# Moving the staged weights of a fused decoder layer by 320 bytes against its activations

## The chip, the core and the metric

The kernel runs on one core of a Trainium2 chip. A core has five engines that run side by side: TensorE multiplies matrices, VectorE and ScalarE work element by element, GpSimd does a few odd jobs, and SyncE here only starts transfers. All read their operands from an on-chip memory of 128 partitions (SBUF); an address below is an offset in bytes along a partition, the same in all 128. TensorE has two kinds of instruction: a weight load (PEld in the rows) reads the stationary operand, a 128x128 block, and a matmul (PE) then reads the moving operand column by column and adds the products into an accumulator memory (PSUM). The metric is device microseconds for one execution, lower being better; the time is the median of several executions.

## What is computed

One layer of a decoder for 512 tokens of width 2048, in float32: a normalisation, one input projection, three token mixers (a gated recurrence A, a sparse attention B, a chunked spatial gating C), one output projection, a second normalisation, and a gated feed-forward part of width 5632 with a short convolution.

```python
h = rms_norm(x, norm_mix)
proj = h @ w_in                                   # 2048 x 6992
a_q, a_f, a_i, a_g, b_q, b_ckv, idx_q, idx_k, idx_w, c_uv = split_cols(proj, IN_SIZES)
out_a = hgrn2_mixer(a_q, a_f, a_i, a_g, lb, a_out_gain)
out_b = dsa_mixer(b_q, b_ckv, idx_q, idx_k, idx_w, w_uk, w_uv, kv_gain, rel_bias)
out_c = gmlp_mixer(c_uv, gmlp_w, gmlp_b)
x = x + concatenate([out_a, out_b, out_c]) @ w_out
h = rms_norm(x, norm_ffn)
a = causal_depthwise_conv3(h @ w_up) + conv_b     # 2048 x 11264
x = x + (silu(a[..., :D_FF]) * a[..., D_FF:]) @ w_down
return rms_norm(x, norm_final)
```

Nearly all of the work is the four matrix products with `w_in`, `w_out`, `w_up` and `w_down`.

## The kernel before

**Tiling.** Activations stand transposed: a tile is 128 features by 512 tokens. Weights come from memory in blocks of 128 by up to 1024 (`stage`, L76): SyncE starts the transfer into `raw`, ScalarE rounds it to `hi` (L82), VectorE makes the rest `lo` (L83). Activations are split into a high and a low part in the same way (`xh`/`xl`, `mh`/`ml`, `hh`/`hl`, `hidh`/`hidl`). Each product of a weight block and an activation tile is then three matmuls (`step`, L94 to 98): high by high, high weights by low activations, low weights by high activations. In `step` the weight block is the stationary operand (128 columns of 4 bytes, 512 bytes of each partition) and the activation tile the moving one (512 columns, 2048 bytes). In `stream` (L204 to 211) it is the other way round: a 128-column slice of the activation tile is stationary and the weights move.

**Stages, in order of time.** The first product (`pia`, weights `wiw`, 336 columns for each of 16 input tiles, L199 to 226) runs while the input arrives. Then come the projections (`proj`, `moving`), between them the three mixers, then the output projection (`wo`), then four groups of the feed-forward part, each with its up-projection (`up`, L793, moving operands `hh`/`hl`) and its down-projection (moving operands `hidh`/`hidl`).

**Addresses.** Tiles are given out by pools, and a pool lies behind the one opened before it. `const` comes first, then `act` (32 tiles of 2048 bytes: `xh`, `xl`, later `mh`, `ml`, `hidh`, `hidl`), `res` (16 tiles of 2048 bytes), `wp` (2 `raw`, 4 `hi`, 4 `lo`, 4096 bytes each), and behind `wp` the pools of the phases: `tp` and `ts` for the mixers, later `hp` (30 of the 32 tiles `hh`/`hl`) and `lp` (`wl_hi`, `wl_lo`). A tile `pad` of 192 bytes in `const` (L183) makes `act` begin at 21504, a multiple of 512. As all sizes up to `ts` are multiples of 512, `act`, `res`, `wp`, `tp`, `hp` and `lp` all begin at a multiple of 512, and so does every 128-column weight block in them. In what follows, the **gap** of a matmul is the start of its moving operand less the start of its stationary one, modulo 512. It is 0 for 10128 of the 10236 matmuls of the split kind. The other 108 are in the first product, where the moving block of an input tile is 1344 bytes wide, so that the blocks of one staged tile begin 0, 1344 and 2688 bytes into it: 60 matmuls have a gap of 320 and 48 one of 128.

```python
PADF = 48
    act = ctx.enter_context(tc.tile_pool(name="act", bufs=1))
    res = ctx.enter_context(tc.tile_pool(name="res", bufs=1))
    wp = ctx.enter_context(tc.tile_pool(name="wp", bufs=1))
    ...
    pad = const.tile([P, PADF], F32, name="pad")
    DVE.memset(pad, 0.0)
```

**Order.** Each engine runs its own instructions in the order in which they stand; waits on other engines are put in by the framework. Staging is given a high priority, so it stands as early as its buffers allow. On TensorE, ten matmuls on a tile of ones (`warm`, L181) stand ahead of the first product.

Of the kernel before, what the change touches and what calls it, by code (L numbers as in the profile page):

```python
# [8 lines left out]
F32 = mybir.dt.float32  # L9
# [6 lines left out]
P = 128  # L16
# [25 lines left out]
U_IQ, U_CKV, U_F, U_Q, U_BQ, U_CU, U_AG = 0, 8, 10, 16, 22, 28, 32  # L42
N_UNITS = 38
NL = 4
PADF = 48

C_NMIX, C_NFFN, C_NFIN, C_LB, C_AGAIN, C_KVG, C_CW, C_CB = 0, 16, 32, 48, 54, 55, 57, 321
N_CONST = 409
# [3 lines left out]
def trunk_kernel(ctx: ExitStack, tc: tile.TileContext, xT, consts, onehot, relb, gw, gb, wk, wv,  # L52
                 wst, wai, wiw, wcv, wo, wu, wd, outT):
    nc = tc.nc
    PE, ACT, DVE, POOL = nc.tensor, nc.scalar, nc.vector, nc.gpsimd

    const = ctx.enter_context(tc.tile_pool(name="const", bufs=1))
    act = ctx.enter_context(tc.tile_pool(name="act", bufs=1))
    res = ctx.enter_context(tc.tile_pool(name="res", bufs=1))
    wp = ctx.enter_context(tc.tile_pool(name="wp", bufs=1))  # L60
    psum = ctx.enter_context(tc.tile_pool(name="psum", bufs=1, space=bass.MemoryType.PSUM))
    dram = ctx.enter_context(tc.tile_pool(name="dram", bufs=1, space=bass.MemoryType.DRAM))

# [116 lines left out]
    for i in range(10):  # L180
        PE.matmul(warm, ones, ones, start=(i == 0), stop=(i == 9))  # L181

    pad = const.tile([P, PADF], F32, name="pad")  # L183
    DVE.memset(pad, 0.0)
    gmx = const.tile([P, KT], F32, name="gmx")
    ACT.dma_start(gmx, consts[:, C_NMIX:C_NMIX + KT])
    for k in range(KT):
# [755 lines left out]
```

## Time and profile before

| | us |
|---|---|
| time, median of 3 runs | 2303.12 (2302.98 to 2303.28) |
| time of the profiled execution | 2303.14 |
| its span, first to last instruction | 2301.4 |
| TensorE busy (matmul) | 2273.6 |
| TensorE busy (weight load) | 1915.3 |
| VectorE busy | 1216.4 |
| ScalarE busy | 878.7 |
| GpSimd busy | 86.1 |

The span is what the instructions of the trace cover; 1.7 us of the profiled execution lie around it. A matmul's duration in the profile (389 ns for 512 columns) covers its whole way through the engine; the next begins long before it ends. What a matmul costs in a dense row of them is the distance from its start to the start of the next, called its **pitch** below. Starts are printed to 0.01 us, so a pitch is best read over many matmuls: by the count in a stretch, or by the first and last start of a row.

### The profile page before, as it was taken

How to read it: one execution, taken by the hardware profiler on the slowest of the kernel's cores; microseconds unless marked ns; L12 is line 12 of the kernel's file. 1: busy time of each engine (PE TensorE's matmuls, PEld its weight loads, DVE VectorE, ACT ScalarE, POOL GpSimd, SP SyncE). 2: the span in 40 equal slices, each digit the busy share in tenths (PEclk: the TensorE clock that was granted, in tenths of full speed). 3: DMA queues.
4: the chain of work that ended last, by engine and by line, in shares of the span. 5: the costliest groups of instructions: out<-in, count | busy, mean ns of one | idle time of the engine just before them, and what ended most of it. 6: DMA issues, size and time to landing. Idle time of an engine off the chain costs nothing.

```text
span 2301.4 us, 27200 instructions
## 1 busy us (share of the span) xinstructions
PE 2273.6 (99%) x10788; PEld 1915.3 (83%) x10788; DVE 1216.4 (53%) x1992; ACT 878.7 (38%) x1272; POOL 86.1 (4%) x150
## 2 busy tenths in 40 slices
PE   8999999999999999999999999999999999999998
PEld 7988889888888888888888888888888888888887
DVE  7689576667675335444334444334544433454446
ACT  6536566755564324333223333222333222333224
POOL 4010000000011110000000000000000000000001
PEclk9999999999999999999999999999999999999999
DMA  5323222222233332332333332333233233323233
GB/s 180 110 89 131 92 78 74 74 71 89 83 124 116 99 98 94 96 97 84 96 107 100 101 97 88 94 98 110 93 100 97 83 95 110 101 94 99 71 113 110
DMA packets 72816, 226.49 MB, mean 98 GB/s; under 512 B 9220, under 2 KB 11674, under 8 KB 72688
## 3 DMA queue, kind: packets, MB, share of 16 engines
q1 hardware_dynamic: 67824, 211.40, 29.3%
q0 software_dynamic: 4720, 13.35, 1.7%
q8 instruction: 84, 1.38, 0.3%
q14 instruction: 44, 0.36, 0.1%
q10 hardware_dynamic: 144, 0.01, 0.0%
HBM read 220.50 MB, written 6.18 MB: 98 GB/s over the span
## 4 chain that ended last, share of the span: by engine, by line
PE 94%; DVE 2%; ACT 2%; DMA 1%; issue 1%; POOL 0%; DVEq 0%; ACTq 0%; POOLq 0%
PE pj L96 24%; PE pj L97 24%; PE pj L98 24%; PE mx L97 3%; PE mx L96 3%; PE mx L98 3%; PE pmv L209 1%; PE pmv L210 1%; PE pmv L211 1%; PE pa L444 1%; ACT hi L82 1%; DMA x<-in_xT_dram 0%; DVE lo L83 0%; PE psc L288 0%; PE ptr L642 0%
## 5 line engine op out<-in xcount | busy, mean ns | idle before, releaser
L82 ACT ACTIVATE hi<-raw 128x1024 fp32r<-128x1024 f32 (+5 forms) x438 | 420.3, 960 | 996.1 <-PE pj L97 764.0
L83 DVE TENSOR_TENSOR lo<-raw,hi 128x1024 fp32r<-128x1024 f32 (+5 forms) x438 | 483.1, 1103 | 459.7 <-ACT hi L82 459.3
L96 PE MATMUL pj<-hh,hi 128*128 128x512 f32 x1408 | 547.8, 389 | 0.0
L98 PE MATMUL pj<-hh,lo 128*128 128x512 f32 x1408 | 547.8, 389 | 0.0
L97 PE MATMUL pj<-hh,hi 128*128 128x512 f32 x1320 | 513.5, 389 | 0.0
L98 PEld LDWEIGHTS pj<-hh,lo 128*128 128x128 f32 x1408 | 264.3, 188 | 54.8
L96 PEld LDWEIGHTS pj<-hh,hi 128*128 128x128 f32 x1408 | 264.3, 188 | 54.7
L97 PEld LDWEIGHTS pj<-hh,hi 128*128 128x128 f32 x1320 | 247.8, 188 | 51.6
L96 PE MATMUL pj<-xh,hi 128*128 128x512 f32 (+1 forms) x608 | 232.2, 382 | 0.9 <-ACT ia L254 0.9
L97 PE MATMUL pj<-xl,hi 128*128 128x512 f32 (+1 forms) x608 | 231.7, 381 | 0.0
L98 PE MATMUL pj<-xh,lo 128*128 128x512 f32 (+1 forms) x608 | 231.0, 380 | 0.0
L787 DVE TENSOR_TENSOR a<-pj,rs 128x512 f32<-128x512 f32 x88 | 60.8, 691 | 291.4 <-PE pj L98 289.4
L96 PEld LDWEIGHTS pj<-xh,hi 128*128 128x128 f32 x608 | 114.2, 188 | 19.2 <-ACT ia L254 1.1
L98 PEld LDWEIGHTS pj<-xh,lo 128*128 128x128 f32 x608 | 114.2, 188 | 18.0
L97 PEld LDWEIGHTS pj<-xl,hi 128*128 128x128 f32 x608 | 114.3, 188 | 17.8
L96 PE MATMUL pj<-hidh,hi 128*128 128x512 f32 x320 | 124.5, 389 | 0.0
L97 PE MATMUL pj<-hidl,hi 128*128 128x512 f32 x320 | 124.5, 389 | 0.0
L98 PE MATMUL pj<-hidh,lo 128*128 128x512 f32 x320 | 124.5, 389 | 0.0
L96 PE MATMUL mx<-hidh,hi 128*128 128x512 f32 x320 | 124.5, 389 | 0.0
L97 PE MATMUL mx<-hidl,hi 128*128 128x512 f32 x320 | 124.5, 389 | 0.0
L98 PE MATMUL mx<-hidh,lo 128*128 128x512 f32 x320 | 124.5, 389 | 0.0
L98 PE MATMUL pj<-mh,lo 128*128 128x512 f32 x256 | 99.9, 390 | 0.0
(340 smaller groups left out, 3007.5 us busy)
## 6 DMA issues: line engine op xcount, KB each, us to landing
raw<-in_wu_dram SPq DMA_DIRECT2D x176, 512.0 KB, 3.6
raw<-in_wst_dram SPq DMA_DIRECT2D x76, 512.0 KB, 3.6
raw<-in_wd_dram SPq DMA_DIRECT2D x48, 384.0 KB, 3.1
raw<-in_wo_dram SPq DMA_DIRECT2D x32, 512.0 KB, 3.7
raw<-in_wd_dram SPq DMA_DIRECT2D x48, 320.0 KB, 2.8
x<-in_xT_dram POOLq DMA_DIRECT2D x32, 256.0 KB, 5.4
raw<-in_wcv_dram SPq DMA_DIRECT2D x8, 512.0 KB, 3.6
raw<-in_wai_dram SPq DMA_DIRECT2D x8, 512.0 KB, 3.7
```

What stands on the lines that cost most here:

```text
L82: ACT.activation(hi[:, :cols], raw[:, :cols], AF.Copy)
L83: DVE.tensor_tensor(lo[:, :cols], raw[:, :cols], hi[:, :cols], op=ALU.subtract)
L96: PE.matmul(ps, wh, ah[:, lo:], start=first, stop=False)
L97: PE.matmul(ps, wh, al[:, lo:], start=False, stop=False)
L98: PE.matmul(ps, wl, ah[:, lo:], start=False, stop=last)
L209: PE.matmul(ps[t], ah[:, ts], wh, start=(k == 0), stop=False)
L210: PE.matmul(ps[t], al[:, ts], wh, start=False, stop=False)
L211: PE.matmul(ps[t], ah[:, ts], wl, start=False, stop=(k == KT - 1))
L444: PE.matmul(pa[:, c * 192:(c + 1) * 192], x[:, cc * P:(cc + 1) * P], y[:, cc * 192:(cc + 1) * 192], start=(c == 0), stop=(c == 1), skip_gr ...
L787: DVE.tensor_tensor(a, ps, rs2, op=ALU.mult)
```

## The change

The tile `pad` goes, so that `act` and `res` begin 192 bytes lower. A tile `shift` of 320 bytes is made the first tile of `wp`, so that `raw`, `hi` and `lo`, and all pools behind them, begin 128 bytes higher than before. In the built program the tiles of `act` and `res` begin at 320 modulo 512, those of `wp`, `tp`, `hp` and `lp` at 128.

```diff
-PADF = 48
+SHIFT = 80
...
     wp = ctx.enter_context(tc.tile_pool(name="wp", bufs=1))
+    shift = wp.tile([P, SHIFT], F32, tag="shift", bufs=1, name="shift")
+    tc.nc.vector.memset(shift, 0.0)
...
-    pad = const.tile([P, PADF], F32, name="pad")
-    DVE.memset(pad, 0.0)
```

| matmuls of the split kind | count | gap before | gap after |
|---|---|---|---|
| `step` with moving operands in `act`: projections, output and down-projections, the last of the 16 tiles of the up-projection | 5160 | 0 | 192 |
| up-projection, the 15 tiles that lie in `hp` | 3960 | 0 | 0 |
| `stream` (activations stationary), first blocks | 660 | 0 | 320 |
| first product, second and third blocks | 60 and 48 | 320 and 128 | 128 and 448 |
| inside the attention (`tp` by `tp` or `wp`) | 348 | 0 | 0 |

All instructions of TensorE, ScalarE, GpSimd and SyncE, with their waits, stand as before. Only the start of VectorE's row differs. Before, it began so (`ones` is the tile for `warm`, L178; the branch ahead of it enters the program):

```order
0 L938 UNCONDITIONAL_BRANCH
1 L178 MEMSET ones 128x128
2 L184 MEMSET pad 128x48
3 L83 TENSOR_TENSOR lo<-raw,hi 128x336
4 L157 SCALAR_TENSOR_TENSOR xl<-x,gmx,xh 128x512
```

In the changed program the same place on VectorE reads:

```order
0 L938 UNCONDITIONAL_BRANCH
1 L62 MEMSET shift 128x80
2 L180 MEMSET ones 128x128
3 L85 TENSOR_TENSOR lo<-raw,hi 128x336
4 L159 SCALAR_TENSOR_TENSOR xl<-x,gmx,xh 128x512
```

The fill of the spacer now stands ahead of `ones` instead of behind it, and is 80 columns wide instead of 48; the line numbers of the next rows are 2 higher, since the file is 2 lines longer up there.

## Rows read from the trace of the kernel before

**Rows 1.** The page: busy time by engine, and shares of the chain that ended last.
```profile
PE 2273.6 (99%) x10788; PEld 1915.3 (83%) x10788; DVE 1216.4 (53%) x1992; ACT 878.7 (38%) x1272; POOL 86.1 (4%) x150
...
PE 94%; DVE 2%; ACT 2%; DMA 1%; issue 1%; POOL 0%; DVEq 0%; ACTq 0%; POOLq 0%
```
**Rows 2.** Stretches: from:to, length, matmul busy (count), granted clock, DMA share, GB/s.
```profile
28.50:30.20 1.70, 1.70 (x7) 0.50 0.37 144
31.00:36.10 5.10, 5.10 (x35) 1.00 0.57 173
```
**Rows 3.** The same view for the feed-forward stretch, 512 columns a matmul.
```profile
1235.00:2230.00 995.00, 995.00 (x4391) 1.00 0.31 95
```
**Rows 4.** TensorE's timeline (start, us, engine, line, operation), 256 columns, weights moving.
```profile
284.79 0.28 PE L211 MATMUL pmv<-lo,xh 128*128 128x256 f32 x1
...
285.99 0.28 PE L209 MATMUL pmv<-hi,xh 128*128 128x256 f32 x1
```
**Rows 5.** TensorE's timeline at the lower clock, first product, 336 columns.
```profile
28.52 0.48 PE L209 MATMUL pia<-hi,xh 128*128 128x336 f32 x1
...
29.92 0.48 PE L211 MATMUL pia<-lo,xh 128*128 128x336 f32 x1
```
**Rows 6.** TensorE's timeline, first product, input tiles 11 to 13, full clock.
```profile
31.07 0.32 PE L209 MATMUL pia<-hi,xh 128*128 128x336 f32 x1
...
32.45 0.31 PE L209 MATMUL pia<-hi,xh 128*128 128x336 f32 x1
...
34.29 0.31 PE L209 MATMUL pia<-hi,xh 128*128 128x336 f32 x1
...
36.13 0.32 PE L209 MATMUL pia<-hi,xh 128*128 128x336 f32 x1
```
**Rows 7.** TensorE's timeline behind a break in the attention, 512 columns.
```profile
581.85 0.40 PE L96 MATMUL pj<-xh,hi 128*128 128x512 f32 x1
582.08 0.40 PE L97 MATMUL pj<-xl,hi 128*128 128x512 f32 x1
582.32 0.40 PE L98 MATMUL pj<-xh,lo 128*128 128x512 f32 x1
582.55 0.39 PE L96 MATMUL pj<-xh,hi 128*128 128x512 f32 x1
```
**Rows 8.** The timeline of the start: VectorE's fills, and what follows them.
```profile
0.90 0.17 DVE L178 MEMSET ones<- 128x128 f32 x1 [0.90 <-PEq L931]
1.02 0.10 DVE L184 MEMSET pad<- 128x48 f32 x1
...
1.12 4.63 PE L181 MATMUL warm<-ones 128*128 128x128 f32 x20 [1.12 <-DVE pad L184]
...
3.74 0.51 DVE L83 TENSOR_TENSOR lo<-raw,hi 128x336 fp32r<-128x336 f32 x1 [2.62 <-ACT hi L82]
...
6.47 0.72 ACT L156 ACTIVATE xh<-x,gmx 128x512 fp32r<-128x512 f32 x1 [2.76 <-DMA x<-in_xT_dram]
...
7.24 0.89 PE L209 MATMUL pia<-hi,xh 128*128 128x336 f32 x4 [1.49 <-ACT xh L156]
```
**Rows 9.** Staging: ScalarE's rounding by line (idle before it), and transfers by median landing.
```profile
L82 ACT ACTIVATE hi<-raw 128x1024 fp32r<-128x1024 f32 (+5 forms) x438 | 420.3, 960 | 996.1 <-PE pj L97 764.0
...
raw<-in_wu_dram SPq DMA_DIRECT2D x176, 512.0 KB, 3.6
raw<-in_wst_dram SPq DMA_DIRECT2D x76, 512.0 KB, 3.6
...
raw<-in_wo_dram SPq DMA_DIRECT2D x32, 512.0 KB, 3.7
```
**Rows 10.** The chain that ended last, in order of time: its long pieces of input transfer.
```profile
4.12 6.57 DMA x<-in_xT_dram
10.98 4.87 DMA x<-in_xT_dram
```

## The prediction

> **What bounds the kernel now.** I read the page's busy times and the shares of the chain first. The reader is to see that TensorE is busy 99% of the span and holds 94% of the chain, while every other engine is at 53% or less [rows 1]. The time is therefore, nearly, the sum of the pitches of some 10,200 matmuls, and the change can matter only if it changes the pitch, or if it delays something early on, where TensorE still waits for input.
>
> Next I read the pitch. In the feed-forward stretch 4391 matmuls of 512 columns begin in 995 us, so the pitch is 995000 / 4391 = 226.6 ns [rows 3]. In a row of matmuls of 256 columns, ten begin between 284.79 and 285.99, so it is 120 ns [rows 4]. The difference, 106.6 ns for 256 columns, is 0.416 ns a column, which is one column a cycle at 2.4 GHz; the granted clock is 1.00 in both kinds of stretch. What is left is the same for both: 226.6 - 213.3 = 13.3 ns, and 120 - 106.7 = 13.3 ns. Call it the **addend**. Over 10,236 matmuls it makes 136 us, 6% of the time.
>
> Then I asked what the addend is. At the lower clock (granted 0.50, which is 1.2 GHz) five matmuls of 336 columns begin between 28.52 and 29.92, 280 ns each [rows 2, 5], and 336 / 1.2 is 280 exactly: there the addend is zero. It is thus no fixed number of cycles of the array. It fits a weight load for the next matmul that disturbs the reading of the moving operand only when that reading runs at full rate, so a quarrel of the two reads can't be excluded from these rows. The change bears on exactly that quarrel: it alters the distance of the two addresses.
>
> **The change, part by part.** *Distance of the reads.* The gap goes from 0 to 192 for 5160 matmuls, from 0 to 320 for 660, stays 0 for 3960 of the up-projection and 348 in the attention, and is permuted for 108. What does a gap other than 0 cost? The trace of before shows three gaps side by side, at full clock [rows 2, 6]. Input tile 11 has the gap 320: nine matmuls from 31.07 to 32.45, 1380 / 9 = 153.3 ns. Tile 12 has 128: twelve from 32.45 to 34.29, 1840 / 12 = 153.3 ns. Tile 13 has 0: twelve from 34.29 to 36.13, 153.3 ns. All three are 140.0 ns for 336 columns and an addend of 13.3. A start is printed to 0.01 us, so each of these means is good to about 1 ns. The addend is the same at gaps 0, 128 and 320, and 320 is 192 on the other side (-192 modulo 512). The gap 192 itself does not occur. The nearest rows are these, and they give zero for it; I take 0 us. The ends: the most that could go is the whole addend, 5160 x 13.3 ns = 69 us; the most that I can find to be added is in the second rival.
>
> [...]
>
> *Start of the weight blocks.* Every weight block in `wp` now begins at 128 modulo 512 instead of 0, and the activation slices that are stationary in `stream` at 320. The 512 bytes of a partition that a weight load reads then cross a multiple of 512, as none of the split kind does now. The three tiles of [rows 6] vary the start of the moving operand (0, 320, 128) and not that of the stationary one, so the trace doesn't show this. From below I see no reason for a gain from it. From above the nearest row of a weight load out of step is that behind a break: three matmuls from 581.85 to 582.55, 233.3 ns each instead of 226.6 [rows 7], 6.7 ns more. I take 0, as the change of the moving operand's start by 320 and by 128, the nearer case, left the pitch as it was; the upper end is the second rival.
>
> *Fills.* The fill of `pad` (0.10 us for 48 columns) goes; one of 80 columns comes ahead of `ones`, between 0.10 and 0.17 us by the two rows that stand there, say 0.13 [rows 8]. The tile `ones` is ready that much later, and `warm`, which begins at 1.12, with it. TensorE then has 1.49 us without work until the first `xh` is there, and that waits 2.76 us for the input's transfer [rows 8]. So this costs 0; without that cover, 0.13 us. VectorE's next instruction, a subtraction for the first weights, comes after 2.62 us of waiting [rows 8], so it isn't moved.
>
> *Transfers.* `raw` begins at 128 instead of 0 modulo 512, the input tiles at 320. A staged block of 1024 columns serves 24 matmuls, 24 x 226.6 ns = 5.4 us, and lands in 3.6 to 3.7 us; ScalarE's 996 us of idle time ahead of the rounding are mostly waits for TensorE to free a buffer (764 us) [rows 9]. So a slower landing is hidden. At the start it isn't: 6.57 and 4.87 us of input transfer lie on the chain [rows 10]. The rows give no price for a changed start; the spread between streams of the same size, 3.6 to 3.7 us, is 3%, and 3% of 11.4 us is 0.3 us either way. I take 0.
>
> *Sum.* 2301.4 + 0 + 0 + 0 + 0, and 1.7 us around the span: 2303.1, which is also the median of the runs shown.
>
> **The rivals.** *First: faster, the quarrel ends at 192.* If two reads meet in the same part of the memory at gaps 0, 128 and 320 but not at 192, the addend goes for 5160 matmuls. For it speaks that the addend vanishes at the lower clock [rows 5], so something is contended; against it that three different gaps gave the same addend to about a nanosecond [rows 6]. It gives 2303 - 69 = 2234 us if all goes, 2269 if half does. It decides from 0.9 ns a matmul (4.6 / 5160).
>
> *Second: slower, weight blocks that cross a multiple of 512 load late.* The place is every weight load of the split kind whose stationary operand begins at 128 or 320 modulo 512, all 10,236; the price at most the 6.7 ns of [rows 7]: 69 us, 2372 us; with 1 ns, 2313 us. It decides from 0.45 ns a load. For it speaks that no row tests the start of the stationary operand; against it that the moving operand's start doesn't matter [rows 6]. The same rival with the gap of 192 as cause would touch the 5160 alone and give at most 35 us, 2338 us.
>
> *Third: the change does less than it says.* The 3960 matmuls of the up-projection keep the gap 0, since `hp` lies behind `wp` and is moved with it. This takes nothing from my forecast, but it is why the first rival counts 5160 and not 10,236, and it makes the up-projection a control.
>
> **How the numbers follow.** About 0.2% (4.6 us) is what a measurement of this kernel can tell from no change. Forecast, no change: 0.80; the start and the odd pitches behind breaks leave a few us on both sides. First rival: 0.09. Second, with either cause: 0.11; a little more than the first, since the stationary start is untested and the gap is tested at three places. The forecast's own range is 2299 to 2307. To hold 8 in 10 it is widened a little to both sides, to the small ends of the rivals (under 1 ns a matmul): 2297 to 2310. Faster 0.09, same 0.80, slower 0.11.
>
> **What would show it.** In the changed kernel's trace the feed-forward stretch should again show 226.6 ns a matmul over some 4390 of them, and its down-projections (gap 192) the same as its up-projections (gap 0). Under the first rival the down-projections fall below 226 ns while the up-projections stay; under the second with the start as cause both rise together, with the gap as cause the down-projections alone. The first product's tiles, then at gaps 320, 128 and 448, should stay at 153.3 ns. `warm` should begin about 0.1 us later, and the first matmul of `pia` still at about 7.2 us. The prediction is wrong if the pitch of any of these kinds moves by 1 ns, or if the start up to 47 us moves by some microseconds.

## The result: 1.1% slower

| | before | after |
|---|---|---|
| time, median, us | 2303.20 (2302.98 to 2303.91) | 2329.20 (2327.12 to 2330.34) |
| span of the profiled execution, us | 2301.4 | 2328.6 |
| TensorE busy (matmul), us | 2273.6 | 2301.7 |

The ratio is 1.0111, with a 95% interval of 1.0094 to 1.0129. The forecast was no change at 2303.1 us, with a range that ended at 2310: wrong. What happened has the place and the sign of the second rival in its other form (the gap of 192 as cause), priced there at up to 35 us.

The page of the changed kernel, busy time by engine and the shares of the chain, answers to [rows 1]:

```profile
PE 2301.7 (99%) x10788; PEld 1914.1 (82%) x10788; DVE 1212.3 (52%) x1992; ACT 879.4 (38%) x1272; POOL 89.3 (4%) x150
...
PE 95%; DVE 2%; ACT 1%; DMA 1%; issue 0%; POOL 0%; DVEq 0%; ACTq 0%; POOLq 0%
```

The bound is the same, and TensorE alone has clearly more to do: 28.1 us more for the same 10788 instructions, while the others change by about 4 us or less. So the pitch has changed. Which one, the costliest groups show (mean duration behind the comma), first of the kernel before and then of the changed one; `hh` are the moving operands of the up-projection, `hidh` those of the down-projections:

```profile
L96 PE MATMUL pj<-hh,hi 128*128 128x512 f32 x1408 | 547.8, 389 | 0.0
...
L96 PE MATMUL pj<-hidh,hi 128*128 128x512 f32 x320 | 124.5, 389 | 0.0
```
```profile
L98 PE MATMUL pj<-hh,hi 128*128 128x512 f32 x1408 | 548.7, 390 | 0.0
...
L98 PE MATMUL pj<-hidh,hi 128*128 128x512 f32 x320 | 126.1, 394 | 0.0
```

The stretches say it as pitches. First the kernel before, then the changed one; of each the first row lies inside a down-projection (gap 0, then 192), the second inside an up-projection (gap 0 in both for 15 tiles of 16), the third in the last part, 256 columns (gap 0, then 192). Columns as in [rows 2]; a stretch counts the matmuls that run in it, up to three more than begin in it.

```profile
1090.00:1200.00 110.00, 110.00 (x487) 1.00 0.34 98
1220.00:1440.00 220.00, 220.00 (x973) 1.00 0.30 95
2243.00:2268.00 25.00, 25.00 (x211) 1.00 0.28 85
```
```profile
1110.00:1220.00 110.00, 110.00 (x473) 1.00 0.33 98
1230.00:1450.00 220.00, 220.00 (x969) 1.00 0.30 95
2271.00:2296.00 25.00, 25.00 (x223) 1.00 0.28 85
```

In the same 110 us there are 14 matmuls fewer in the down-projection, 4 of 973 fewer in 220 us of the up-projection (whose sixteenth tile lies in `act` and has the gap 192), and 12 more in 25 us of the last part. From the first and last start of each stage the pitches are 226.67 and 233.33 ns in the down-projections, and 119.97 and 113.38 ns over the first 240 matmuls of the last part: 6.67 ns more at 512 columns and 6.6 less at 256, at the same gap of 192 and the same granted clock of 1.00.

Summed over every start in the two traces, what a pitch has beyond its columns' own time (0.4167 ns each, an estimate from the two pitches of before: 226.67 less 119.97 ns over 256 columns) and 13.3 ns (taking only matmuls with less than 20 ns of it, the others being waits) is 2.2 us before and 29.9 us after. These 27.7 us are the loss; the span grew by 27.2, so that all else (the start, the waits) comes to -0.5 us together.

### The profile page after: what moved, and what is told of

Same layout as the page of the kernel before. It is cut to its first block, busy times and chain, and to the rows that moved or that the text cites. A ratio compares the mean times of both kernels' runs of the same rounds, so it can differ in the third digit from the quotient of the medians.

```text
span 2328.6 us, 27200 instructions
## 1 busy us (share of the span) xinstructions
PE 2301.7 (99%) x10788; PEld 1914.1 (82%) x10788; DVE 1212.3 (52%) x1992; ACT 879.4 (38%) x1272; POOL 89.3 (4%) x150
## 4 chain that ended last, share of the span: by engine, by line
PE 95%; DVE 2%; ACT 1%; DMA 1%; issue 0%; POOL 0%; DVEq 0%; ACTq 0%; POOLq 0%
PE pj L99 25%; PE pj L98 25%; PE pj L100 25%; PE mx L100 3%; PE mx L99 3%; PE mx L98 3%; PE pmv L209 1%; PE pmv L210 1%; PE pmv L211 1%; PE pa L444 1%; DMA x<-in_xT_dram 1%; ACT hi L84 0%; PE psc L288 0%; PE ptr L642 0%; PE pj L845 0%
```

## The experiments

Three theories stood at the start. **G**: the gap alone sets the pitch. **M** and **S**: what counts is where the moving operand, or the weight block, begins. The changed kernel moves all three. Runs of the kernel before, made beside each experiment, gave medians of 2304.1 to 2304.3 us. Where lines of code are left out, `...` stands for them.

### Each half of the change by itself

The first half, as an edit of the kernel before:

```diff
-PADF = 48
...
-    pad = const.tile([P, PADF], F32, name="pad")
-    DVE.memset(pad, 0.0)
```

> Half of the change: the tile pad goes, no tile shift is put in. All tiles and weight blocks then begin at 320 modulo 512, and the gap between moving and stationary operand is 0 as before. Theory G (the gap alone sets the pitch): as before, 2303 us (2302 to 2305), 226.7 ns for 512 columns everywhere. Theory S (weight blocks that cross a multiple of 512 are slow): slower by up to 26 us, all kinds of matmuls alike. Theory M (moving operands that begin at 320 are slow): the projections and down-projections at 233 ns as in the changed kernel, about 2329 us.

Measured: 2304.46 us, ratio 1.0001 (0.9992 to 1.0011). Next the other half, as an edit of the changed kernel, without the spacer and with two existing tiles in its place:

```diff
-SHIFT = 80
...
-    shift = wp.tile([P, SHIFT], F32, tag="shift", bufs=1, name="shift")
-    tc.nc.vector.memset(shift, 0.0)
+    mv = wp.tile([P, NT, CG, 2], F32, tag="mv", bufs=1, name="mv")
+    va = wp.tile([P, 3, NT, CG], F32, tag="va", bufs=1, name="va")
...
-        mv = small([P, NT, CG, 2], "mv", 1)
...
-        va = small([P, 3, NT, CG], "va", 1)
```

(The tile `pad` is gone here as well, which together with the two tiles puts the activations back to a multiple of 512.)

> The other half: the activation tiles begin at 0 modulo 512 as before, the weights and all behind them at 320 (two small tiles of statistics, 320 bytes together, stand in front of the weights instead of a spacer). The gap is 192 in the same 5160 matmuls as in the changed kernel, and the up-projection keeps 0. Theory G: as the changed kernel, 2329 us (2326 to 2332), 233.3 ns in the down-projections and 226.7 in the up-projections. Theory M: 2303 us, since moving operands begin at 0 again. Theory S: all matmuls alike, the up-projections too.

Measured: 2328.13 us, ratio 1.0101 (1.0084 to 1.0118). The same three stretches, of the first half and then of the second:

```profile
1095.00:1205.00 110.00, 110.00 (x487) 1.00 0.34 100
1220.00:1440.00 220.00, 220.00 (x972) 1.00 0.29 95
2245.00:2270.00 25.00, 25.00 (x211) 1.00 0.27 85
```
```profile
1105.00:1215.00 110.00, 110.00 (x473) 1.00 0.32 95
1230.00:1450.00 220.00, 220.00 (x969) 1.00 0.30 95
2270.00:2295.00 25.00, 25.00 (x223) 1.00 0.27 85
```

487, 972, 211 is the picture of before; 473, 969, 223 that of the changed kernel. The first half has every tile and every weight block at 320 and loses nothing, so M and S fall. (For S the changed kernel says the same: its up-projections read weights that begin at 128, and 15 of 16 tiles lose nothing.) The second has the activations at 0 and a gap of 192 and loses 24.0 of the 26.0 us. So of the three it is G that accounts for the loss.

The gap is not the whole rule, though. The 192 matmuls of 512 columns in which the weights move have a gap of 320 in the changed kernel and in the second half alike. The same 33 us of them, in the kernel before (gap 0), the changed kernel and the second half:

```profile
145.00:178.00 33.00, 33.00 (x148) 1.00 0.34 102
```
```profile
145.00:178.00 33.00, 33.00 (x143) 1.00 0.32 94
```
```profile
145.00:178.00 33.00, 33.00 (x146) 1.00 0.35 102
```

By the starts these are 226.7, 233.3 and 228.9 ns. The same gap and width gave two pitches here; whether the starts themselves or what ran ahead make the difference was not tested. Over 192 matmuls it is 0.8 us.

### Which gaps cost

Each unit of a down-projection has its own staged weights, and its buffer of 1024 columns is wider than the at most 768 that a unit fills. So one kernel can hold every gap, by writing the weights of unit d further on in the buffer (`oh`, `ol` in columns of 4 bytes, for the high and the low halves; the lines that hand them on to `stage` are left out here):

```diff
...
-            w = tiles_of(wd[gidx * KT + d], FT)
+            oh, ol = [(8 * d, 8 * d), (8 * d + 4, 8 * d + 4), (0, 8 * d)][gidx]
+            w = tiles_of(wd[gidx * KT + d], FT, oh, ol)
...
-        w = tiles_of(wd[(FG - 1) * KT + d], FT - NL)
+        w = tiles_of(wd[(FG - 1) * KT + d], FT - NL, 8 * d, 0)
```

> The kernel before, with the staged weights of each down-projection unit written at another place in their buffer (16 units in each of four groups). Group 1: the place moves by 32 bytes a unit, so the gap runs over 16 values; group 2: the same 16 bytes further on; group 3: only the low halves of the weights move; group 4 (first part): only the high halves. In the last part (256 columns) the blocks move by 32 bytes a unit too. Theory G: at a place of 320 (gap 192) 233.3 ns as in the changed kernel, at 0 226.7 ns, and between them steps of 64 bytes, since all pitches so far are multiples of 6.67 ns, the time of 16 columns or 64 bytes; in group 3 a third of the loads are moved, so a third of the effect. A rival, that any gap but 0 costs 6.7 ns, would give 233 ns at all other places. For 256 columns G expects 113.3 ns at gap 192 and 120 at 0. The total time says little here: within 2295 to 2315 us.

The timeline of TensorE, first matmul of consecutive units (33 matmuls each) in group 1: the units at the places 0 and 32, then 224 (its start alone), 256, 288 and 320:

```profile
1089.19 0.39 PE L97 MATMUL pj<-hidh,hi 128*128 128x512 f32 x1
1096.68 0.39 PE L97 MATMUL mx<-hidh,hi 128*128 128x512 f32 x1
1104.38 0.40 PE L97 MATMUL pj<-hidh,hi 128*128 128x512 f32 x1
...
1142.73 0.40 PE L97 MATMUL mx<-hidh,hi 128*128 128x512 f32 x1
1150.43 0.39 PE L97 MATMUL pj<-hidh,hi 128*128 128x512 f32 x1
1157.92 0.39 PE L97 MATMUL mx<-hidh,hi 128*128 128x512 f32 x1
1165.62 0.40 PE L97 MATMUL pj<-hidh,hi 128*128 128x512 f32 x1
1173.32 0.39 PE L97 MATMUL mx<-hidh,hi 128*128 128x512 f32 x1
```

7.49 us / 33 is 227 ns at places 0 and 256, 7.70 / 33 is 233.3 at 32, 224, 288 and 320. A place of p bytes is a gap of -p modulo 512: place 320 is gap 192, place 192 is gap 320. From the second to the 32nd start of each unit, in ns:

| place, bytes | 0 | 32 | 64 | 96 | 128 | 160 | 192 | 224 | 256 | 320 |
|---|---|---|---|---|---|---|---|---|---|---|
| 512 columns | 226.7 | 233.2 | 233.3 | 234.1 | 232.2 | 233.3 | 229.0 | 233.3 | 226.7 | 233.3 |

The row repeats after 256 bytes to a tenth of a ns; in group 2 the places 16 and 272 give 226.7, 240 and 496 give 227.3, and all others 230 or more. No place tried gave less than the 226.7 ns of gap 0. With only the low halves moved, a third of the loads, the pitches at the places that cost are still 231 to 233 ns, not a third of the way: that expectation failed, as did the steps of 64 bytes. And "any gap but 0 costs" failed at the places 16 and 256. The last part, whose place changes every 12 matmuls, gave 116.7 to 120.0 ns and not the 113.3 of the changed kernel at the same gap; that stayed open here. The time of this kernel, one run, is 2312.87 us.

One more kernel puts the period to the total time: the changed kernel with a spacer of 256 bytes.

```diff
-    shift = wp.tile([P, SHIFT], F32, tag="shift", bufs=1, name="shift")
-    tc.nc.vector.memset(shift, 0.0)
+    wp.tile([P, 64], F32, tag="shift", bufs=1, name="shift")
```

> The changed kernel with a spacer of 256 bytes instead of 320 in front of the weights, so that the gap is 256 in the 5160 matmuls. If the pattern repeats every 256 bytes, as the sweep has it: 226.7 ns everywhere and 2303 to 2304 us, as before. If it is 512 bytes, or any gap but 0 costs: 233.3 ns in the projections and down-projections, about 2329 us.

Measured: 2304.37 us, ratio 1.000 (0.9991 to 1.001), and 226.67 ns in the down-projections and up-projections, the first two stretches:

```profile
1095.00:1205.00 110.00, 110.00 (x487) 1.00 0.35 100
1220.00:1440.00 220.00, 220.00 (x972) 1.00 0.30 94
```

So a gap of 256 cost nothing here, where one of 192 cost 6.67 ns a matmul and 26 us in all.

### Why the first product showed nothing

[Rows 6] had given the same pitch at gaps 0, 128 and 320. They differ from the rest of the kernel in two ways: 336 columns instead of 512, and weights that move. In group 1 (gap 192) and group 2 (gap 0) of this kernel the columns were cut, unit by unit, and in group 3 the weight columns:

```diff
...
+            oh = ol = [80, 0, 0 if d < 8 else 80][gidx]
+            n, m = (T - 16 * d, P) if gidx < 2 else (T, P // 2)
...
-            accumulate([ps], [w], hid)
+            accumulate([ps[:m, :n]], [[(a[:, :m], b[:, :m]) for a, b in w]], [(a[:, :n], b[:, :n]) for a, b in hid])
```

> Leaves out a part of the down-projections: in group 1 (weights at place 320, gap 192) and group 2 (place 0, gap 0) unit d multiplies only the first 512 - 16 d columns; in group 3 only 64 of the 128 weight columns of each block are used, at place 0 in units 0 to 7 and at 320 in units 8 to 15. It asks why the first product (336 columns) showed nothing. Theory G (what is added depends on the gap and on the width together, because the width decides where the next pair of reads meets): group 1 is at 20 ns over the columns' own time at 512, near 13.3 around 336 to 384, and falls below 13.3 towards 272; group 2 stays at 13.3. A rival, that the first product is immune because there the weights move and the activations stand still: 20 ns at all widths of group 1. If the weight reads are what is added, 64 weight columns add half: 6.7 ns at place 0.

Timeline, first matmul of units in group 1: 512 columns up to the second row, 496 up to the third; then the unit with 336; then the unit with 336 in group 2; then, in group 3, one with 64 weight columns at place 0 and one at place 320.

```profile
1088.20 0.40 PE L97 MATMUL pj<-hidh,hi 128*128 128x512 f32 x1
...
1095.90 0.39 PE L97 MATMUL mx<-hidh,hi 128*128 128x496 f32 x1
...
1103.16 0.38 PE L97 MATMUL pj<-hidh,hi 128*128 128x480 f32 x1
...
1159.28 0.32 PE L97 MATMUL mx<-hidh,hi 128*128 128x336 f32 x1
...
1164.34 0.31 PE L97 MATMUL pj<-hidh,hi 128*128 128x320 f32 x1
...
1492.29 0.32 PE L97 MATMUL mx<-hidh,hi 128*128 128x336 f32 x1
...
1497.35 0.31 PE L97 MATMUL pj<-hidh,hi 128*128 128x320 f32 x1
...
1807.75 0.39 PE L97 MATMUL mx<-hidh,hi 128*64 128x512 f32 x1
...
1815.34 0.40 PE L97 MATMUL pj<-hidh,hi 128*64 128x512 f32 x1
...
1823.02 0.39 PE L97 MATMUL mx<-hidh,hi 128*64 128x512 f32 x1
```

With 33 matmuls a unit, that is 233.3 and 220.0 ns, then 153.3 for 336 columns at either gap, then 230.0 and 232.7. Less the columns' own time at the estimated 0.4167 ns each, the addend in ns, at all widths that ran:

| columns | 512 | 496 | 480 | 464 | 448 | 432 | 416 | 400 | 384 | 368 | 352 | 336 | 320 | 304 | 288 | 272 |
|---|---|---|---|---|---|---|---|---|---|---|---|---|---|---|---|---|
| gap 192 | 20.0 | 13.3 | 16.0 | 19.7 | 15.5 | 13.6 | 13.3 | 16.7 | 16.7 | 15.6 | 13.3 | 13.3 | 13.3 | 12.0 | 13.4 | 10.1 |
| gap 0 | 13.3 | 13.3 | 16.7 | 16.7 | 16.0 | 15.6 | 15.2 | 13.5 | 14.2 | 13.4 | 13.3 | 13.3 | 13.3 | 11.2 | 11.8 | 12.2 |

At 336 columns a gap of 192 makes no difference even with the weights standing still, and at 512 it makes 6.67 ns. So it is the width that made [rows 6] blind, and the rival falls. Theory G has its parts that failed, too: at gap 192 the addend is 16.7 and not near 13.3 at 384, and at gap 0 it does not stay at 13.3. The changed kernel says the same of the width from the other side: the 512-column matmuls in which the weights move have the gap 320 there, one that [rows 6] had cleared, and their pitch is 233 ns as well (0.70 us for three, from 149.64 to 150.34); in the sweep the same gap, place 192, cost 2.3 ns:

```profile
149.64 0.40 PE L210 MATMUL pmv<-hi,xl 128*128 128x512 f32 x1
149.87 0.40 PE L211 MATMUL pmv<-lo,xh 128*128 128x512 f32 x1
150.10 0.40 PE L209 MATMUL pmv<-hi,xh 128*128 128x512 f32 x1
150.34 0.40 PE L210 MATMUL pmv<-hi,xl 128*128 128x512 f32 x1
```

Nor is every gap free at 336 columns. In the first product of the changed kernel twelve matmuls with gap 128 begin from 38.94 on, and twelve with gap 448 from 40.78 to 42.65:

```profile
38.94 0.32 PE L209 MATMUL pia<-hi,xh 128*128 128x336 f32 x1
...
40.78 0.32 PE L209 MATMUL pia<-hi,xh 128*128 128x336 f32 x1
...
42.65 0.28 PE L131 MATMUL pcol<-ones,xacc 128*128 128x1 f32 x2
```

That is 153.3 and then 155.8 ns, where the prediction had 153.3 for all three gaps. (Nine more with gap 448, from 35.72 to 37.10, stay at 153.3.)

With 64 weight columns the addend at place 0 is 16.7 ns, more than with 128, not half. The thought that the bytes of the weight read are simply added to the time falls too. The addend doesn't shrink smoothly with the width in either row of the table: at gap 192 it is 13.3 ns at 496 columns and 19.7 at 464, at gap 0 13.3 and 16.7. That the width decides where two reads meet, the reason that Theory G gave, no run shows. (This kernel does less work; one run took 2254.0 us.)

### Gaps that stay, and two rhythms

> The kernel before, with the staged weights of the down-projections at one place for a whole group of 16 units: 192 bytes in group 1, 240 in group 2, 224 in group 3, 64 in the first part of group 4 (gaps 320, 272, 288 and 448). In the sweep these places gave 229.0, 227.3, 233.3 and 233.3 ns after a change of place at each unit. Theory H (the two reads fall into a rhythm that depends on how they met, so a place that stays may settle elsewhere): group 1 moves off 229.0, to 226.7 or to 233.3. Theory G (the place alone decides): the same figures as in the sweep within 0.5 ns. No group below 226.7 ns by either. Time 2303 to 2312 us.

The edit is `oh = ol = [48, 60, 56][gidx]` (16 in group 4). One run took 2311.92 us. One stretch inside each of the first three groups:

```profile
1095.00:1205.00 110.00, 110.00 (x482) 1.00 0.34 100
1455.00:1565.00 110.00, 110.00 (x487) 1.00 0.34 100
1815.00:1925.00 110.00, 110.00 (x474) 1.00 0.33 96
```

By the starts: 228.9, 226.7, 233.3 and, in group 4, 233.3 ns. Three agree with the sweep; place 240 settles at 226.7 instead of 227.3, 0.6 ns, just over what G allowed. Theory H had said that group 1 would move, and it did not. For the 512 columns of the down-projections the run speaks for G. For 256 columns it is otherwise, as the next two show. The first puts a gap of 192 into the last part alone; the second does this too (the line is not shown again) and also sets the unit ahead of it at place 320.

```diff
     lp = ctx.enter_context(tc.tile_pool(name="lp", bufs=1))
+    lp.tile([P, 80], F32, name="gap", tag="gap", bufs=1)
```

> The kernel before, with 320 unused bytes in front of the two large weight tiles of the last part only (384 matmuls of 256 columns), so that only these have the gap 192. The changed kernel and the second half showed 113.3 ns there instead of 120. Theory G: 384 x 6.67 ns = 2.6 us less than before, 2301 us, a ratio of 0.9989. If the 113.3 ns depend on how the stretch is entered (theory H), anything from 0 to 2.6 us.

```diff
...
-        w = tiles_of(wd[(FG - 1) * KT + d], FT - NL)
+        w = tiles_of(wd[(FG - 1) * KT + d], FT - NL, 80 if d == KT - 1 else 0)
```

> As e6 (gap 192 in the last 384 matmuls), and the one staged unit ahead of them (21 matmuls of 512 columns) stands at place 320 too, so that the last part is entered from the 233 ns rhythm instead of the 226.7 ns one. Theory H (with the same addresses there are two rhythms, and the entry picks one): 113.3 ns in the last part as in the changed kernel, which is 384 x 6.67 ns = 2.6 us less, and 21 x 6.67 ns = 0.1 us more for the unit: about 2.5 us faster than before, ratio 0.9989. Theory G (the addresses alone decide): 117.7 ns as in e6, 0.8 us faster.

The last part, same 25 us, of the first kernel and then of the second:

```profile
2243.00:2268.00 25.00, 25.00 (x215) 1.00 0.27 85
```
```profile
2243.00:2268.00 25.00, 25.00 (x223) 1.00 0.28 85
```

215 and 223, against 211 before; by the starts over 240 matmuls 117.78 and 113.36 ns, against 119.97. The addresses in the last part are the same in both kernels. What differs is the unit of 21 matmuls ahead, and the rhythm is kept for 240 matmuls, up to a break by short sums. Behind a second break, 26 matmuls later, 11 us of the remaining 118 matmuls are, in the first kernel and then in the second:

```profile
2276.00:2287.00 11.00, 11.00 (x100) 1.00 0.50 192
```
```profile
2275.00:2286.00 11.00, 11.00 (x96) 1.00 0.50 191
```

Now the first runs at 113.4 ns and the second at 117.8: each has changed over to the other's rhythm, at the same gap. So with one set of addresses there are two rhythms, 117.8 and 113.4 ns, and the entry decides: H holds here as far as the pitches go. That two reads meet, its reason, no run shows. This is also why the expected 2.6 us could not come: in neither kernel do all 384 matmuls gain 6.6 ns. The times are 2302.99 us, ratio 0.9995 (0.9986 to 1.0004), and 2302.10 us, ratio 0.9992 (0.9983 to 1.0001). Both medians are lower, in the order expected, but the intervals reach 1: by the total time neither can be told from no change, and only the trace shows the gain in its stretch.

## Why the prediction was wrong

*What bounds the kernel* and *the pitch*: right. TensorE was the bound before and after, and a change of the pitch by 1 ns was named as what would make the forecast wrong; it was 6.67. The 2.4 GHz in that step is an estimate and not a clock that the profile gives: it is 1 / 0.416 ns, by the pitches of [rows 3, 4], if a column takes a cycle, and 1.2 GHz is its half, by the granted 0.50 [rows 2].

*Distance of the reads*: here it failed. The step took an addend from 336-column rows [rows 6] to 512-column matmuls, "the nearest rows", and called them good to 1 ns. They were, for 336 columns at the gaps 0, 128 and 320. The pitch depends on the gap and the width together, and 336 happens to be a width at which these gaps, and 192 with the weights standing still, make no difference. The rows had the addend the same for 256 and 512 columns at gap 0 alone [rows 3, 4]; that it stays so at other gaps was taken over without a row. (By their count in the trace the three tiles of [rows 6] are the tiles 8 to 10, counted from 0, and not 11 to 13; their gaps are as stated.) The term should have been 4392 matmuls of 512 columns x 6.67 ns = 29 us, 192 in which the weights move x 6.1 ns = 1 us, less up to 3 us in the 256-column parts; the 384 of 384 columns hardly count. That is 27 us, where it said 0.

*The end of that term.* Upwards it pointed to the second rival, 6.7 ns a matmul from the odd pitches behind a break [rows 7]; with the gap as cause that is 35 us and 2338, against the 2329 that came. The price was thus at hand and right to 0.1 ns, and the range still ended at 2310, because the chance was put at 0.11 with both causes together. That the price agreed was luck: [rows 7] stand at gap 0, and the row there is back at 226.7 ns after some ten matmuls. Nor was a weight load out of step there: in the trace of before the loads for the next matmul begin at 581.85, 582.08 and 582.32, each together with a matmul of [rows 7], as they do further on in the same row at 226.7 ns a matmul (584.16, 584.39 and 584.84). [Rows 7] were matmuls of 512 columns with a pitch above 226.7 at full clock; they showed that this kind can run in a slower rhythm, and as an end of the range deserved more weight than a row of another width.

*Start of the weight blocks*: right, 0. With all at 320 and gap 0 the time is 2304.46 against 2304.1.

*Fills*: right. `warm` begins at 1.21 instead of 1.12, hidden by the wait behind it (2.27 us, before 1.49); the first matmul of `pia` begins at 7.72 instead of 7.24, and between 6.82 and 8.12 in the five experiments whose addresses up to there are those of before:

```profile
0.89 0.12 DVE L62 MEMSET shift<- 128x80 f32 x1 [0.89 <-PEq L931]
0.99 0.17 DVE L180 MEMSET ones<- 128x128 f32 x1
...
1.21 0.58 PE L183 MATMUL warm<-ones 128*128 128x128 f32 x1 [1.21 <-DVE ones L180]
```

*Transfers*: not shown wrong. The start was 2.1 us longer in this profile (the first short sums on TensorE, `pcol`, begin at 42.65 instead of 40.60), but in the same five experiments this point lies between 40.50 and 42.07, so it says little.

*The first rival* (the addend goes at 192) was wrong for 512 columns and half right for 256: in the last part 6.6 of 13.3 ns go for 240 matmuls, and about 2 ns for the rest. *The third*, that the up-projection keeps its gap and is a control, was right, and made the cause visible at first sight.

*The quarrel of the two reads*, which the first rival rested on, was the author's estimate from the zero addend at the granted clock 0.50 [rows 5]. No run shows it. What the runs show at 512 columns in the down-projections is 226.67 ns at gap 0 and 233.33 at gap 192.

## What to carry to other kernels

Where TensorE is the bound with 512-column matmuls of this split float32 kind, keep the start of the moving operand and that of the stationary one at the same address modulo 256, in every pool: here the places of group 1 of the sweep, all but 0 and 256, cost 2.3 to 7.4 ns of the 226.7 (those of 16 and 240 bytes in group 2 none and 0.6), and the gap of the change 1.1% of the time. A spacer or a tile of odd size in one pool moves everything behind it, so look at the distance, not at the pool. And an addend measured at one width need not hold at another (at gap 192 it was 13.3 ns at 336 columns and 20.0 at 512): a term for 512 columns needs a row of 512 columns, and where there is none the end of the range has to hold the worst pitch seen at that width.

## What was not expected of the hardware

- In the down-projections, 512 columns, the pitch repeats with the gap every 256 bytes: 226.7 ns with the weights 0, 16 or 256 bytes further on, and 240 where they stay there; 229 to 234 at the other places tried.
- The gap alone does not give it: with the weights moving, the same gap of 320 took 233.3 ns in one kernel and 228.9 in another.
- The same gap of 192 costs 6.67 ns at 512 columns, nothing at 336 with the weights standing still (153.3 ns at either gap), and saves up to 6.6 at 256.
- With the same addresses 256-column matmuls run at 117.8 or at 113.4 ns, by what ran just ahead of them, for 240 matmuls on end, and change over behind a break.
- A weight block of 64 columns gave a longer pitch (230.0 ns at gap 0) than one of 128 (226.7).

What makes the pitch depend on all this was not settled, nor why 336 columns take 280 ns at the granted clock 0.50 [rows 5], twice 140.0 and no addend: the runs show a dependence on gap, width, weight columns and entry, and no rule that gives them all.
